# Mixer AB of a two-block network: order of the chunk-begin tables, engine of the chunk recurrence, place of the third responses

## The chip, the cores and the metric

One core of a Trainium2 chip runs the whole program. The metric is the time of one execution on the device in microseconds; the median of three runs of the kernel before is 2368.24 us.

## The reference, cut to what matters

Two blocks run one after the other on a sequence of 512 tokens with 1024 features. The first block has two layers; its layer 0 begins with the mixer below. The change touches only this mixer, and in it only the state-space part `s5_ssm` and the gates of the mLSTM part.

```python
def mixer_ab(x, ...):
    proj = x @ w_in                       # xm | zm | us, 512 columns each
    xc = silu(causal_dwconv(xm, conv_w, conv_b))
    q, k, v = block-diagonal products of xc, xc, xm
    gates = concatenate([q, k, v]) @ w_if + b_if
    h = mlstm_chunkwise(q, k, v, gates[:4], gates[4:])
    out_m = (layernorm(h) * mh_gain + skip * xc) * silu(zm)
    y = gelu(s5_ssm(us, ...))
    out_s = y * sigmoid(y @ w_glu + b_glu)
    return concatenate([out_m, out_s]) @ w_out

def s5_ssm(u, ...):                       # 32 groups of 64 complex states
    x[t] = ab * x[t-1] + bb @ u[t]        # ab, bb from a, dt, b
    y[t] = re(c @ x[t]) + d * u[t]
```

## The kernel before, in words

Every projection is made of three TensorE passes in a split format: a weight tile `raw` of 128x1024 is loaded by the SP queue (three buffers), ScalarE rounds it to `wh` (line 142), VectorE takes the rest `wl = raw - wh` (line 145), and lines 269 to 271 multiply. `fill(zm, n)` runs n steps of three such matmuls of the projection `zm`; the mixer puts them between its small products.

The state-space part cuts the 512 tokens into 64 chunks of 8. It needs two sets of tables, both products of powers of `ab` (`par`, `pai`) with `b` or `c`:

- `end_state_tables` (line 891) makes `zr`, `zi` on VectorE, four groups of four columns of groups. Per group, six instructions of 128x512: two products into a PSUM tile `aux`, two into `zr` and `zi`, and two sums. The powers lie in PSUM too (tile `chain`), so each instruction has at least one input in PSUM.
- `start_state_tables` (line 909) makes `cr`, `ci` on POOL in two halves. Per half, six instructions of 128x1152 with both inputs in SBUF (four products, two sums), and a negation on ScalarE. They read the reversed powers `pcr`, `pci`, which ScalarE copies out of `par`, `pai`.

Then `end_transpose` and `end_states` (lines 923 and 933) turn `zr`, `zi` on TensorE and give every chunk's end state `X`, in four groups; `conv` (line 987) makes one quarter of `xc` beside each: a ScalarE instruction, three VectorE instructions with both inputs in SBUF (`ta`), a ScalarE Silu. The work tiles `ta` have two buffers, shared by the turned tables and the convolution. `scan` (line 945) is the recurrence over the 64 chunks: on POOL, 28 instructions of 128x256 inside blocks of eight chunks, 28 of 128x32 across the blocks (`cy`), and then twelve VectorE and four POOL instructions that make the chunks' begin states `Xp`.

`responses` (line 995, four calls) multiplies `cr`, `ci` with `zr`, `zi` on TensorE (32 matmuls) and has ScalarE copy the result to `hs`, of which there is one buffer: `hs0` for calls 0 and 1, `hs1` for calls 2 and 3. `toeplitz` (line 1009, two calls) adds the skip weights on VectorE and spreads `hs` by 16 transfers on the SP queue into `Mt`. `block_diag` makes the block-diagonal weights `bd` with twelve VectorE instructions, in the buffer that `zr` had. The heads come behind: `head_decay` (decay weights `wt`), `values`, `queries_keys`, `head_scores`, `head_b`, `head_c`, and between them `ssm_out`, which reads `Mt`, `Xp`, `cr`, `ci`.

TensorE's order in the mixer is the order of the program, written out by hand (`manual_schedule`). On the other engines a planner orders the instructions: it walks a timeline of its own, and each engine takes the first in the program among those ready. `issue_after(ins)` makes the instructions traced under it stand behind `ins` on the engine of `ins`. The program's order around the change is: `xm` projection, end and start tables, chunk powers on POOL, first step of `zm`, the four groups with the convolution, `scan`, responses 0, gate matmuls (line 1201, which read all four quarters of `xc`), gate arithmetic, responses 1, `toeplitz(0)`, running sum and maximum of the gates (`fr`, `mr`, lines 1232 and 1234), gate transposes (lines 1241, 1242), responses 2 and 3, `toeplitz(1)`, `block_diag`, the last fills, heads.

Of the kernel before, what the change touches and what calls it, by code (L numbers as in the profile page):

```python
# [131 lines left out]
def tile_blocks(ctx: ExitStack, tc: tile.TileContext, A: dict, P: dict, off: dict, cst: bass.AP, out: bass.AP):  # L132
# [11 lines left out]
    def tt(out, a, b, op=ALU.mult, eng=None):  # L144
        return (eng or V).tensor_tensor(out=out, in0=a, in1=b, op=op)  # L145
# [24 lines left out]
    def chain_tile():  # L170
        return aux_p.tile([128, 512], F32, tag="chain", name="chain", bufs=1)
# [509 lines left out]
    def mixer_ab(scr_u):  # L681
        W = A["ab_w_in"][0]
        with tc.tile_pool(name="ab", bufs=1) as mp, tc.tile_pool(name="abt", bufs=2) as tp:
            def slot(i, shape, nm, dt=F32):
                return mp.tile(shape, dt, tag=f"s{i}", name=nm)
# [61 lines left out]
            def block_diag(out, nm):  # L747
                wr = vpart(nm).rearrange("p (m e) -> p m e", m=4)
                for m in range(4):
                    tt(out[:, m].rearrange("p (n e) -> p n e", e=4), blk4.rearrange("p (n e) -> p n e", e=4),  # L750
                       wr[:, m:m + 1, :].to_broadcast([128, 32, 4]))
# [17 lines left out]
            with tc.issue_after(last_split.ins):  # L769
# [51 lines left out]
                def powers(eng, pr, pi, order):  # L821

                    for t in (1, 2, 4):
                        cmul(eng, pr[:, :, order(t + 1, 2 * t + 1)], pi[:, :, order(t + 1, 2 * t + 1)],
                             pr[:, :, order(1, t + 1)], pi[:, :, order(1, t + 1)],
                             b_(pr[:, :, order(t, t + 1)], t), b_(pi[:, :, order(t, t + 1)], t), pt1[:, :, 0:t], pt2[:, :, 0:t])
# [63 lines left out]
            def end_state_tables():  # L890


                pw = chain_tile()[:, 0:288].rearrange("p (i j t) -> p i j t", i=2, j=16)
                act(pw[:, 0], par)
                act(pw[:, 1], pai)
                bbr, bbi, b1, b2 = (s5b[:, 1024 + i * 256:1280 + i * 256].rearrange("p (j q) -> p j q", q=16) for i in range(4))
                g16r, g16i = (b_(c.rearrange("p (j a) -> p j a", a=1), 16) for c in (gr, gi))
                cmul(V, bbr, bbi, bre, bim, g16r, g16i, b1, b2)
                for b4 in range(4):
                    js = slice(b4 * 4, b4 * 4 + 4)  # L900
                    pr, pi = pw[:, 0, js, 1:9], pw[:, 1, js, 1:9]
                    for z, p0, p1, op in ((zr, pr, pi, ALU.subtract), (zi, pi, pr, ALU.add)):
                        t = aux_tile().rearrange("p (j q s) -> p j q s", j=4, q=16)
                        outer(V, t, bbi[:, js], p1, 8, True)
                        outer(V, z[:, js], bbr[:, js], p0, 8, True)
                        tt(z[:, js], z[:, js], t, op)

            def start_state_tables():

                for hj in range(2):  # L910
                    eng = G
                    tc_ = slot(8 + hj, [128, 8, 9, 16], "tc")
                    js = slice(hj * 8, hj * 8 + 8)
                    outer(eng, cr[:, js], cre[:, js], pcr[:, js], 9, False)
                    outer(eng, tc_, cim[:, js], pci[:, js], 9, False)
                    tt(cr[:, js], cr[:, js], tc_, ALU.subtract, eng=eng)
                    outer(eng, ci[:, js], cre[:, js], pci[:, js], 9, False)
                    outer(eng, tc_, cim[:, js], pcr[:, js], 9, False)
                    tt(ci[:, js], ci[:, js], tc_, ALU.add, eng=eng)
                    act(ci[:, js], ci[:, js], scale=-1.0)  # L920
# [23 lines left out]
            def scan():  # L944

                Xv = X.rearrange("p i j (b r) -> p i j b r", r=8)
                a8s = mp.tile([128, 2, 16], F32, name="a8s")
                ts(a8s[:, 0], pwi[:, :, 1], -1.0, eng=G)
                G.tensor_copy(out=a8s[:, 1], in_=pwi[:, :, 1])
                sh = [128, 2, 16, 8]  # L950
                A8r = pwr[:, :, 1:2].rearrange("p (i j) b -> p i j b", i=1).to_broadcast(sh)
                A8i = a8s.rearrange("p i (j b) -> p i j b", b=1).to_broadcast(sh)
                sct = ev.tile([128, 512], F32, tag="sq", name="sct")
                t, u = (sct[:, i * 256:(i + 1) * 256].rearrange("p (i j b) -> p i j b", i=2, j=16) for i in range(2))
                for r in range(1, 8):
                    tt(t, Xv[:, :, :, :, r - 1], A8r, eng=G)
                    tt(u, Xv[:, ::-1, :, :, r - 1], A8i, eng=G)
                    tt(t, t, u, ALU.add, eng=G)
                    tt(Xv[:, :, :, :, r], Xv[:, :, :, :, r], t, ALU.add, eng=G)
                cy = ev.tile([128, 2, 16, 8], F32, tag="rbm", name="cy")  # L960
                G.memset(cy[:, :, :, 0], 0.0)
                w1, w2 = t[:, :, :, 0], u[:, :, :, 0]
                p8s = mp.tile([128, 2, 16], F32, name="p8s")
                ts(p8s[:, 0], pwi[:, :, 8], -1.0, eng=G)
                G.tensor_copy(out=p8s[:, 1], in_=pwi[:, :, 8])
                p8r = pwr[:, :, 8:9].rearrange("p j i -> p i j").to_broadcast([128, 2, 16])
                for b in range(1, 8):
                    tt(w1, cy[:, :, :, b - 1], p8r, eng=G)
                    tt(w2, cy[:, ::-1, :, b - 1], p8s, eng=G)
                    tt(w1, w1, w2, ALU.add, eng=G)  # L970
                    tt(cy[:, :, :, b], w1, Xv[:, :, :, b - 1, 7], ALU.add, eng=G)
                for hj in range(2):
                    js = slice(hj * 8, hj * 8 + 8)
                    for i in range(2):
                        Xp[i, hj] = resid.tile([128, 8, 64], F32, tag=f"xh{4 + i * 2 + hj}", name=f"Xp{i}{hj}")
                        o = Xp[i, hj].rearrange("p j (b r) -> p j b r", r=8)
                        t = sct.rearrange("p (j b r) -> p j b r", j=8, b=8)
                        cyr, cyi = (cy[:, c, js].rearrange("p j (b a) -> p j b a", a=1).to_broadcast([128, 8, 8, 8]) for c in range(2))
                        pr, pi = (w[:, js, 0:8].rearrange("p j (a r) -> p j a r", a=1).to_broadcast([128, 8, 8, 8])
                                  for w in ((pwr, pwi) if i == 0 else (pwi, pwr)))  # L980
                        tt(o, cyr, pr)
                        tt(t, cyi, pi, eng=G)
                        tt(o, o, t, ALU.subtract if i == 0 else ALU.add)
                        tt(o[:, :, :, 1:8], o[:, :, :, 1:8], Xv[:, i, js, :, 0:7], ALU.add)

            def conv(m):
                cw, cb = cols["ab_conv_w"], cols["ab_conv_b"]
# [161 lines left out]
            with tc.manual_schedule(engines={T.engine}):  # L1149
# [5 lines left out]
                ci = slot(5, [128, 16, 9, 16], "ci")  # L1155
                pc = ev.tile([128, 3, 16, 9], F32, tag="sq", name="pc")
                pcr, pci, pwr = (pc[:, i] for i in range(3))
                for t in range(9):
                    act(pcr[:, :, t], par[:, :, 8 - t])
                    act(pci[:, :, t], pai[:, :, 8 - t])  # L1160
                with tc.issue_after(last_split.ins):
                    end_state_tables()
                    start_state_tables()

                G.memset(pwr[:, :, 0], 1.0)
                G.memset(pwi[:, :, 0], 0.0)
                G.tensor_copy(out=pwr[:, :, 1], in_=par[:, :, 0])
                G.tensor_copy(out=pwi[:, :, 1], in_=pai[:, :, 0])
                powers(G, pwr, pwi, lambda lo, hi: slice(lo, hi))
                sz = slot(7, [128, 4, 512], "sz")  # L1170
                zm = proj_fine([(W, 512 + c * 128, ev_zm(c)) for c in (0, 2)], xh, xl, KD)

                def fill(gen, n):
                    for _ in range(n):
                        next(gen, None)
# [7 lines left out]
                for b4 in range(4):  # L1183
                    conv(b4)
                    end_states(b4)
                    if b4 < 3:
                        end_transpose(b4 + 1)
                        fill(zm, 2)
                scan()


                Mt = [slot(8 + i, [128, 16, 128], f"Mt{i}") for i in range(2)]
# [43 lines left out]
                tt(er, fr, mr, ALU.add)  # L1236
                ts(mr, mr, -1.0)
                fill(zm, 4)
                ps = chain_tile()
                for tb in range(NT):  # L1240
                    T.transpose(ps[:, tb * 4:tb * 4 + 4], cr4[:, tb * 128:(tb + 1) * 128], ident[0:4, 0:4])
# [2 lines left out]
                em = mp.tile([128, NT, 4], F32, name="em")  # L1244
                V.tensor_copy(out=cc.rearrange("p a b -> p (a b)"), in_=ps[:, 0:16])
                act(em.rearrange("p a b -> p (a b)"), ps[:, 16:32], AF.Exp, scale=-1.0)
                hsl[1] = mp.tile([128, 8, 8, 16], F32, tag="hs", name="hs1")
                responses(2)
                fill(zm, 2)
                responses(3)  # L1250
                toeplitz(1)
                bd = slot(0, [128, 3, 4, 128], "bd")
                for i, nm in enumerate(("ab_wv", "ab_wq", "ab_wk")):
                    block_diag(bd[:, (2, 0, 1)[i]], nm)
                q = [resid.tile([128, 512], F32, tag=f"xh{m}", name=f"q{m}") for m in range(4)]
                kk_ = [resid.tile([128, 512], F32, tag=f"xl{m}", name=f"k{m}") for m in range(4)]
                v = slot(1, [128, 2112], "v")[:, 0:NT * 516].rearrange("p (t m e) -> p t m e", t=NT, m=4)
# [620 lines left out]
```

## Time and profile before

| what | us |
|---|---|
| median of 3 runs (2367.17 to 2369.4) | 2368.24 |
| the profiled execution | 2366.72 |
| its span, first to last instruction | 2364.6 |
| TensorE busy in the span | 2309.1 (98%) |
| VectorE busy | 1363.6 (58%) |
| ScalarE busy | 1033.1 (44%) |
| POOL busy | 461.6 (20%) |

The profile is of one execution. PE is TensorE, DVE VectorE, ACT ScalarE, POOL GpSimd, SP the queue of loads. Times are counted from the first instruction. Busy shares are averages over the span; a stage is read from the stretch where it lies. The mean granted clock of TensorE is 0.994 of 2.4 GHz.

### The profile page before, as it was taken

How to read it: one execution, taken by the hardware profiler on the slowest of the kernel's cores; microseconds unless marked ns; L12 is line 12 of the kernel's file. 1: busy time of each engine (PE TensorE's matmuls, PEld its weight loads, DVE VectorE, ACT ScalarE, POOL GpSimd, SP SyncE). 2: the span in 40 equal slices, each digit the busy share in tenths (PEclk: the TensorE clock that was granted, in tenths of full speed). 3: DMA queues.
4: the chain of work that ended last, by engine and by line, in shares of the span. 5: the costliest groups of instructions: out<-in, count | busy, mean ns of one | idle time of the engine just before them, and what ended most of it. 6: DMA issues, size and time to landing. Idle time of an engine off the chain costs nothing.

```text
span 2364.6 us, 30936 instructions
## 1 busy us (share of the span) xinstructions
PE 2309.1 (98%) x12106; PEld 1929.7 (82%) x12106; DVE 1363.6 (58%) x2054; ACT 1033.1 (44%) x1583; POOL 461.6 (20%) x519
## 2 busy tenths in 40 slices
PE   9799999999999999999999999999999999999999
PEld 7558888888878888888888778888888878888888
DVE  8675744432657556444228675777533775777722
ACT  4545533222568554323235664444323573444411
POOL 5831400001401132000017562000002662000000
PEclk9899999999999999999999999999999999999999
DMA  6212333323332223333334103333234203333332
GB/s 189 62 22 71 99 98 99 98 90 112 107 89 72 72 90 99 97 94 95 98 98 132 57 28 98 101 96 98 94 98 120 82 2 98 98 98 98 94 116 94
DMA packets 204609, 216.04 MB, mean 91 GB/s; under 512 B 11888, under 2 KB 189936, under 8 KB 204464
## 3 DMA queue, kind: packets, MB, share of 16 engines
q1 hardware_dynamic: 204464, 214.08, 29.4%
q8 instruction: 95, 1.56, 0.3%
q14 instruction: 50, 0.41, 0.1%
HBM read 209.72 MB, written 3.15 MB: 90 GB/s over the span
## 4 chain that ended last, share of the span: by engine, by line
PE 83%; DVE 7%; POOL 4%; ACT 3%; issue 2%; DMA 0%; SPq 0%; DVEq 0%; ACTq 0%; POOLq 0%
PE mm L271 21%; PE mm L269 21%; PE mm L270 21%; PE mm L313 5%; PE mm L445 2%; PE mm L446 2%; PE mm L447 2%; DVE wl L145 1%; DVE xl L148 1%; PE aux L1662 1%; PE chain L1686 1%; POOL ra L145 1%; PE mm L1641 1%; ACT L142 1%; ACT wh L142 1%
## 5 line engine op out<-in xcount | busy, mean ns | idle before, releaser
L145 DVE TENSOR_TENSOR wl<-raw,wh 128x1024 fp32r<-128x1024 f32 (+1 forms) x396 | 492.0, 1243 | 615.8 <-ACT wh L142 614.8
L142 ACT ACTIVATE wh<-raw 128x1024 fp32r<-128x1024 f32 (+1 forms) x396 | 411.7, 1040 | 721.2 <-PE mm L270 525.4
L269 PE MATMUL mm<-xh,wh 128*128 128x512 f32 x1536 | 602.1, 392 | 0.5 <-ACT xh L142 0.5
L270 PE MATMUL mm<-xl,wh 128*128 128x512 f32 x1536 | 599.2, 390 | 2.4 <-DVE xl L148 2.4
L271 PE MATMUL mm<-xh,wl 128*128 128x512 f32 x1536 | 598.7, 390 | 2.1 <-DVE wl L145 2.0
L270 PEld LDWEIGHTS mm<-xl,wh 128*128 128x128 f32 x1536 | 289.1, 188 | 63.4 <-DVE xl L148 4.2
L271 PEld LDWEIGHTS mm<-xh,wl 128*128 128x128 f32 x1536 | 288.9, 188 | 63.0 <-DVE wl L145 3.0
L269 PEld LDWEIGHTS mm<-xh,wh 128*128 128x128 f32 x1536 | 289.1, 188 | 62.0 <-issue 1.7
L145 POOL TENSOR_TENSOR acc<-acc,sq 128x256 f32<-128x256 f32 (+1 forms) x77 | 86.6, 1124 | 418.9 <-issue 263.7
L145 POOL TENSOR_TENSOR accm<-accm,sq 128x512 f32<-128x512 f32 (+1 forms) x24 | 32.1, 1338 | 677.3 <-ACT sq L142 677.0
L148 DVE SCALAR_TENSOR_TENSOR y<-cbuf,vec,y 128x512 f32<-128x512 f32 x176 | 131.1, 748 | 38.0 <-ACT y L142 35.9
L445 PE MATMUL mm<-wh,xh 128*128 128x512 f32 (+1 forms) x384 | 147.7, 385 | 0.1
L446 PE MATMUL mm<-wh,xl 128*128 128x512 f32 (+1 forms) x384 | 143.9, 375 | 0.0
L447 PE MATMUL mm<-wl,xh 128*128 128x512 f32 (+1 forms) x384 | 143.8, 375 | 0.0
L270 PE MATMUL mm<-bl,wh 128*128 128x512 f32 x308 | 119.8, 389 | 0.0
L269 PE MATMUL mm<-bh,wh 128*128 128x512 f32 x308 | 119.8, 389 | 0.0
L271 PE MATMUL mm<-bh,wl 128*128 128x512 f32 x308 | 119.8, 389 | 0.0
L142 ACT ACTIVATE y<-cbuf,vec 128x512 f32<-128x512 f32 x88 | 71.4, 813 | 98.5 <-DVE cbuf L145 96.5
L269 PE MATMUL mm<-gh,wh 128*128 128x512 f32 x264 | 102.7, 389 | 0.0
L271 PE MATMUL mm<-gh,wl 128*128 128x512 f32 x264 | 102.7, 389 | 0.0
L270 PE MATMUL mm<-gl,wh 128*128 128x512 f32 x264 | 102.7, 389 | 0.0
L145 DVE TENSOR_TENSOR t<-mm,rb 128x512 f32<-128x512 f32 (+1 forms) x92 | 58.4, 642 | 58.7 <-PE mm L271 58.4
(465 smaller groups left out, 3847.1 us busy)
## 6 DMA issues: line engine op xcount, KB each, us to landing
raw<-in_ffn_w SPq DMA_DIRECT2D x136, 512.0 KB, 3.6
raw<-in_w_up SPq DMA_DIRECT2D x88, 512.0 KB, 3.5
raw<-in_w_down SPq DMA_DIRECT2D x43, 512.0 KB, 3.5
raw<-in_c_w_in SPq DMA_DIRECT2D x33, 512.0 KB, 3.8
raw<-in_w_in SPq DMA_DIRECT2D x31, 512.0 KB, 3.7
raw<-in_w_o SPq DMA_DIRECT2D x16, 512.0 KB, 3.6
raw<-in_ab_w_in SPq DMA_DIRECT2D x11, 512.0 KB, 5.0
raw<-in_ab_w_out SPq DMA_DIRECT2D x9, 512.0 KB, 3.6
```

Of the source, the lines that this page charges most:

```text
L142: S.activation(out=out, in_=in_, func=func, scale=scale, **kw)
L145: return (eng or V).tensor_tensor(out=out, in0=a, in1=b, op=op)
L148: return V.scalar_tensor_tensor(out=out, in0=a, scalar=s, in1=b, op0=op0, op1=op1)
L269: T.matmul(ps, h, xh, start=first, stop=False)
L270: T.matmul(ps, h, xl, start=False, stop=False)
L271: T.matmul(ps, l, xh, start=False, stop=last)
L313: T.matmul(o, w[:, k, m * 128:(m + 1) * 128], x, start=k0 == mine[0] and k == 0 and p == 0, stop=k0 == mine[-1] and k == nk - 1 and p == 2)
L445: T.matmul(o, xh[:, sl], wh[:, k, :], start=first, stop=False)
L446: T.matmul(o, xl[:, sl], wh[:, k, :], start=False, stop=False)
L447: T.matmul(o, xh[:, sl], wl[:, k, :], start=False, stop=last)
L1641: T.matmul(sc, qT[:, h, sl], kT[c][:, h // 4, :], start=c == 0, stop=c == 1)
L1662: T.transpose(pt[:, kb * 128:(kb + 1) * 128], p[:, kb * 128:(kb + 1) * 128], ident)
```

## The change

Four edits, all in the mixer. The chunk powers on POOL stand ahead of the start tables in the program, and the end tables are traced first; the last of the nine columns of `pcr` and `pci` is no longer copied by ScalarE but by two VectorE copies that stand behind the last end-table instruction, so that POOL's first table product, which reads all nine, waits for them. The 56 instructions of the recurrence run on VectorE in place of POOL. The third responses (call 2) and their buffer come ahead of the gate transposes on TensorE. The second Toeplitz and the block diagonals stand behind the last instruction of the recurrence on VectorE.

```diff
@@ end_state_tables
-                        tt(z[:, js], z[:, js], t, op)
+                        last = tt(z[:, js], z[:, js], t, op)
+                return last
@@ scan
                 for r in range(1, 8):
-                    tt(t, Xv[:, :, :, :, r - 1], A8r, eng=G)
-                    tt(u, Xv[:, ::-1, :, :, r - 1], A8i, eng=G)
-                    tt(t, t, u, ALU.add, eng=G)
-                    tt(Xv[:, :, :, :, r], Xv[:, :, :, :, r], t, ALU.add, eng=G)
+                    tt(t, Xv[:, :, :, :, r - 1], A8r)
+                    tt(u, Xv[:, ::-1, :, :, r - 1], A8i)
+                    tt(t, t, u, ALU.add)
+                    tt(Xv[:, :, :, :, r], Xv[:, :, :, :, r], t, ALU.add)
...
                 for b in range(1, 8):
-                    tt(w1, cy[:, :, :, b - 1], p8r, eng=G)
-                    tt(w2, cy[:, ::-1, :, b - 1], p8s, eng=G)
-                    tt(w1, w1, w2, ALU.add, eng=G)
-                    tt(cy[:, :, :, b], w1, Xv[:, :, :, b - 1, 7], ALU.add, eng=G)
+                    tt(w1, cy[:, :, :, b - 1], p8r)
+                    tt(w2, cy[:, ::-1, :, b - 1], p8s)
+                    tt(w1, w1, w2, ALU.add)
+                    carried = tt(cy[:, :, :, b], w1, Xv[:, :, :, b - 1, 7], ALU.add)
...
+                return carried
@@ mixer_ab
-                for t in range(9):
+                for t in range(8):
                     act(pcr[:, :, t], par[:, :, 8 - t])
                     act(pci[:, :, t], pai[:, :, 8 - t])
-                with tc.issue_after(last_split.ins):
-                    end_state_tables()
-                    start_state_tables()
 
                 G.memset(pwr[:, :, 0], 1.0)
                 G.memset(pwi[:, :, 0], 0.0)
                 G.tensor_copy(out=pwr[:, :, 1], in_=par[:, :, 0])
                 G.tensor_copy(out=pwi[:, :, 1], in_=pai[:, :, 0])
+                with tc.issue_after(last_split.ins):
+                    last_end = end_state_tables()
                 powers(G, pwr, pwi, lambda lo, hi: slice(lo, hi))
+
+                with tc.issue_after(last_end.ins):
+                    V.tensor_copy(out=pcr[:, :, 8], in_=par[:, :, 0])
+                    V.tensor_copy(out=pci[:, :, 8], in_=pai[:, :, 0])
+                start_state_tables()
...
-                scan()
+                carried = scan()
...
                 fill(zm, 4)
+                hsl[1] = mp.tile([128, 8, 8, 16], F32, tag="hs", name="hs1")
+                responses(2)
                 ps = chain_tile()
...
                 act(em.rearrange("p a b -> p (a b)"), ps[:, 16:32], AF.Exp, scale=-1.0)
-                hsl[1] = mp.tile([128, 8, 8, 16], F32, tag="hs", name="hs1")
-                responses(2)
                 fill(zm, 2)
                 responses(3)
-                toeplitz(1)
                 bd = slot(0, [128, 3, 4, 128], "bd")
-                for i, nm in enumerate(("ab_wv", "ab_wq", "ab_wk")):
-                    block_diag(bd[:, (2, 0, 1)[i]], nm)
+                with tc.issue_after(carried.ins):
+                    toeplitz(1)
+                    for i, nm in enumerate(("ab_wv", "ab_wq", "ab_wk")):
+                        block_diag(bd[:, (2, 0, 1)[i]], nm)
```

## Rows read from the trace of the kernel before

**Rows 1.** Stretches: length, each engine's busy time (instructions), granted clock, DMA share, GB/s
```profile
58.00:72.00 14.00, 5.84 (x26) 3.87 (x26) 14.00 (x13) 2.85 (x4) 14.00 (x9) 0.63 0.23 76
...
68.30:71.50 3.20, 3.18 (x10) 2.57 (x10) 3.20 (x3) 0.60 (x1) 3.20 (x3) 0.51 0.11 38
...
136.30:139.80 3.50, 3.50 (x5) 1.51 (x6) 3.03 (x7) 1.21 (x4) 1.55 (x3) 0.52 0.00 0
```
**Rows 2.** TensorE's waits between 36 and 150 us: total, times, longest
```profile
PE aux L927 <- DVE zr L145: 5.5, 1, 5.5
PE chain L1242 <- DVE fr L145: 4.1, 1, 4.1
PE aux L1025 <- DVE wt L145: 2.4, 2, 1.3
PE mm L271 <- DVE wl L145: 2.0, 1, 2.0
PE chain L1201 <- ACT xc L142: 0.9, 1, 0.9
...
PE aux L927 <- DVE zi L145: 0.7, 1, 0.7
```
**Rows 3.** Timeline of VectorE, 35 to 70 us: start, length
```profile
35.75 0.22 DVE L145 TENSOR_TENSOR pt<-par 128x64 f32<-128x64 f32 x1
...
36.02 0.42 DVE L145 TENSOR_TENSOR s5b<-s5b 128x256 f32<-128x256 f32 x1
...
38.38 2.29 DVE L145 TENSOR_TENSOR s5b<-s5b 128x256 f32<-128x256 f32 x1
40.59 2.17 DVE L145 TENSOR_TENSOR pai<-pt,pt 128x64 f32<-128x64 f32 x1
42.68 1.21 DVE L145 TENSOR_TENSOR wl<-raw,wh 128x1024 fp32r<-128x1024 f32 x1
...
48.60 2.95 DVE L145 TENSOR_TENSOR wl<-raw,wh 128x1024 fp32r<-128x1024 f32 x1
...
57.45 3.03 DVE L145 TENSOR_TENSOR wl<-raw,wh 128x1024 fp32r<-128x1024 f32 x1
...
62.80 3.08 DVE L145 TENSOR_TENSOR wl<-raw,wh 128x1024 fp32r<-128x1024 f32 x1
...
68.79 0.67 DVE L145 TENSOR_TENSOR zi<-zi,aux 128x512 f32<-128x512 f32 x1
```
**Rows 4.** Groups of POOL by form, 36 to 145 us: count, busy, mean ns
```profile
L145 POOL TENSOR_TENSOR tc<-s5b,pc 128x1152 f32<-128x1152 f32 x4 | 8.5, 2140 | 0.0
...
L145 POOL TENSOR_TENSOR ci<-ci,tc 128x1152 f32<-128x1152 f32 x2 | 5.2, 2631 | 0.0
```
**Rows 5.** Groups of VectorE by form, 36 to 145 us
```profile
L145 DVE TENSOR_TENSOR aux<-s5b,chain 128x512 f32<-128x512 f32 x8 | 5.5, 681 | 0.0
...
L145 DVE TENSOR_TENSOR lg<-lg,le 128x16 f32<-128x16 f32 x1 | 0.7, 712 | 0.0
```
**Rows 6.** Timeline of VectorE, 72 to 130 us
```profile
72.37 0.74 DVE L148 SCALAR_TENSOR_TENSOR ta<-xm,vec,ta 128x512 f32<-128x512 f32 x1
...
85.73 3.21 DVE L148 SCALAR_TENSOR_TENSOR ta<-xm,vec,ta 128x512 f32<-128x512 f32 x3
...
115.97 3.87 DVE L145 TENSOR_TENSOR bd<-blk,vec 128x128 f32<-128x128 f32 x12 [0.28 <-PE aux L1003]
...
129.48 0.75 DVE L145 TENSOR_TENSOR Xp<-cy,pc 128x512 f32<-128x512 f32 x1 [1.16 <-POOL cy L145]
```
**Rows 7.** Timeline of POOL: the recurrence's second and last instruction
```profile
87.18 1.21 POOL L145 TENSOR_TENSOR sct<-X,a8s 128x256 f32<-128x256 f32 x1
...
129.14 0.30 POOL L145 TENSOR_TENSOR cy<-sct,X 128x32 f32<-128x32 f32 x1
```
**Rows 8.** Timeline of ScalarE: the last quarter of xc
```profile
88.97 0.63 ACT L142 ACTIVATE xc<-ta 128x512 f32<-128x512 f32 x1 [1.14 <-DVE ta L148]
```
**Rows 9.** The chain that ended last: the third responses
```profile
109.32 3.36 PE aux L1003 x32
```

## The prediction

> **What bounds the kernel now.** TensorE is busy for 98% of the span (the table above), so time can be won only where it waits or runs at its lower clock, and the change touches the stretch from 36 to 148 us alone. I read that stretch in four views. The stretches with their granted clock come first [rows 1]: between 58 and 72 us TensorE has 5.8 us of work in 14.0. TensorE's waits say who ended them [rows 2]: the first hole is a wait for the weight split `wl` (2.0) and for VectorE's chunk-end tables `zr` (5.5, and 0.7 more for `zi`); the second is the gate's running sums (`fr`, 4.1). Two smaller ones are the causal convolution's last `xc` (0.9) and, among the heads, the decay weights `wt` (2.4 in two waits, the longer 1.3). After two of these the granted clock is 0.51 and 0.52, which is 1.2 GHz, for 3.2 and 3.5 us [rows 1].
>
> VectorE's timeline says why the tables are late [rows 3]. The split of 128x1024 takes 1.21 us, but three of them in the tables' stretch take 2.95 to 3.08, one 128x256 product 2.29 instead of 0.42, one 128x64 sum 2.17 instead of about 0.22. Each has both inputs in SBUF and meets one of POOL's 128x1152 instructions (2.14 to 2.63 us, twelve of them in the chunk-begin tables) [rows 4]. The chunk-end tables' own instructions take an input from PSUM; their eight `aux` products take 0.68 us in the mean, with POOL busy beside them [rows 5]. So today POOL's tables lie beside VectorE work that mostly does not feel them.
>
> **The change, part by part**
>
> *POOL waits for VectorE.* Five stretched instructions lose their wait: 1.9 + 1.9 + (2.95 + 3.03 + 3.08 - 3 x 1.21 = 5.4) = 9.2 us. The last table instruction then starts at 59.6 instead of 68.79 [rows 3] and ends at 60.2. TensorE is through its xm products at 58 in either kernel, where the hole begins, so it would lose 8.2 us of waits (2.0 + 5.5 + 0.7) and 1.6 us of slow clock (half of 3.2 [rows 1]): 9.8 us on offer. POOL's 18 small power instructions run earlier beside PSUM-fed work, and two of 18 ScalarE copies become two VectorE copies of 16 columns: nothing, at most 0.4 us.
>
> *What is late next.* POOL's twelve table instructions start at about 60.4: 8 x 2.14 + 4 x 2.63 = 27.7 us if alone. Beside them VectorE now has the convolution: twelve 128x512 `ta` instructions and a split `wl`, all with two SBUF inputs. Alone a `ta` takes 0.74 us; three beside POOL's short 128x256 instructions took 3.21, and one of POOL's between them 1.21: they take turns [rows 6, 7]. Against 128x1152 instructions each `ta` waits 2.14 to 2.63 first. In turns: the split to 61.5, POOL's 27.7, eleven instructions of 0.65 between them (7.2), the last `ta` 0.74 and ScalarE's 0.63 for `xc`: the last `xc` at 97.8 instead of 89.6 [rows 8]. Fewer turns give 96.5, another split in the row 99.5. All gate matmuls stand behind that `xc` on TensorE, whose order is fixed; so the 9.8 us on offer are not kept, and the gate comes **8.2 us later** (6.9 to 9.9). The first responses wait for POOL's first six table instructions and ScalarE's negation, at 60.4 + 1.1 + 13.9 + 5 x 0.65 = 79 at the earliest; that lies under the longer wait.
>
> The Trainium skill, SBUF — State Buffer, section "Who interferes with whom", says the shared pair goes to whichever instruction starts first and "Issue order, not op shape, decides who blocks". Read so that VectorE's queued instructions keep the pair, the convolution would run at 0.74 us each and the sum would be that of the first rival; the rows of turn-taking above speak against that reading.
>
> *Clock.* TensorE now waits 0.9 us before the gate [rows 2]; it would come there up to 9.8 earlier and leave 8.2 later, so it idles some 10 us. The nearest rows cost 1.6 and 1.7 us of half rate after a hole [rows 1]; ends 0 and 1.7. **+1.6**.
>
> *Recurrence on VectorE.* POOL loses 56 instructions, spread from before 87.2 to 129.4 [rows 7]. No row shows them on VectorE. The near rows are the 128x256 product (0.42) and a 128x64 one (0.22) [rows 3]; most need the one before, so no overlap: 28 x 0.42 + 28 x 0.22 = 18 us, between 12 (all at 0.22) and 24 (all at 0.42). They follow the convolution, from 97 to about 122 with other work between, so they share VectorE with the gate's ten small instructions. Each of these may stand behind one recurrence instruction, up to 0.4 each (+4), and no longer meets POOL's 128x256 ones (a sum of 16 columns, `lg`, took 0.71 [rows 5], 0.5 more than the 0.22 of 64 columns; for six such, -3). **+1** (-3 to +4).
>
> *Third responses in the gate gap.* 32 matmuls, two ScalarE copies, no DMA. They take 3.36 us at half clock behind the gap [rows 9], so 1.7 in it at full clock, under the 4.1 us wait. What is left of the gap, some 3 us, is still more than the 1.3 us after which the clock fell among the heads [rows 1, 2], so I let the slow stretch move to what follows. **-1.7** (0 if the gap has closed; -3.4 if the clock stays up). The two copies must wait until the first Toeplitz transfers have read the one `hs` buffer; they hold one `aux` bank meanwhile, and nobody needs the result before the second Toeplitz.
>
> *Second Toeplitz and block diagonals behind the recurrence.* The block diagonals already wait for the fourth responses (they start at 115.97, 3.87 us for twelve) [rows 6] and would start at about 122 to 124 in either case; the cover is the last fill of TensorE, about 5 us; without it up to 4 us. The 16 Toeplitz transfers stay in front of the output-weight loads on SP, as now, and these are needed only after the heads. **0** (to +4).
>
> *Heads.* The chunk states' twelve `Xp` instructions leave the stretch from 129.48 on [rows 6], where they stand between the decay weights: waits of 2.4 and half clock for 3.5 us (1.7) [rows 1, 2]. They now run at some 122 to 131, before the first `wt` product. **-3.5** of 4.1 (0 to -4.1).
>
> *Sum*: 8.2 + 1.6 + 1 - 1.7 - 3.5 = **+5.6 us**. Made against the profiled execution: 2366.7 + 5.6 = 2372.3; the median of the runs (2368.24) stands 1.5 above that execution, so **2373.8** for a median. Work behind the heads is bound by TensorE and moves with it. The bounds together give -4 (6.9 + 0 - 3 - 3.4 - 4.1) to +20 (9.9 + 1.7 + 4 + 0 + 4 + 0), neither end likely whole; the likeliest case by itself is 2367 to 2380. What a measurement of this kernel can tell from no change is about 0.2%, or 4.7 us.
>
> **The rivals**
>
> *VectorE keeps the port (faster).* If its back-to-back instructions go first and POOL only fits in between, the convolution is hidden as now, the first responses come at 76 and the gate at about 80. Then -9.6 + 1 - 1.7 - 3.5 = -13.8: 2354. The Trainium skill's sentence on issue order, named above, is what would allow it. For it: nothing in the rows is an exact pair of a 128x512 `ta` and a 128x1152 table instruction. Against it: the turns in [rows 6, 7] and the one whole wait of each split [rows 3]. It decides at the mean time of a `ta`: (97.8 - 0.6 - 61.5) / 12 = 2.97 us in my sum, break-even 5.6 us earlier, at 2.5, and faster beyond the limit of measurement under 2.1. Chance 0.18, halves of it included.
>
> *The gate queues behind the whole recurrence (slower still).* The planner orders VectorE by program order among what it takes to be ready, and the recurrence stands ahead of the gate. The gate's first VectorE instruction, `ga`, would be asked for at about 104 (some 6 us of matmuls behind `xc` at 97.8); behind all 56 it runs at 97 + 18 = 115. About +10 more: 2384. For it: the program order. Against it: in the profile VectorE's order mixes chains, since a dependent instruction leaves room for another. Chance 0.15.
>
> *The waits do nothing.* The wait on the recurrence may be idle, as the block diagonals wait anyway. The wait of POOL can't be: the two copies feed POOL's first product. So the whole edit is not without effect, but its parts can cancel (gate +6.9, clock +1.6, heads -4.1, gap -3.4): +1, about 2369. That is the forecast's lower part and gets no chance of its own.
>
> **How the numbers follow.** Forecast 0.67, of which 0.37 lies more than 4.7 us above, 0.28 within, 0.02 below. The first rival gives 0.18 faster; the second 0.13 slower and 0.02 within. Faster 0.20, same 0.30, slower 0.50. The range leaves out a tenth at each end: the lower part of the first rival, and the end of the second: 2360 to 2381.
>
> **What would show it.** Right: the three splits at 1.2 us and the last `zi` at 60; TensorE's 5.5 us wait for `zr` gone; twelve `ta` of 2.5 to 3.3 us between POOL's table instructions; the largest wait of the stretch now at the gate matmuls, for `xc`, 8 to 14 us, ending at 96 to 100; the wait for `fr` shorter by 1.7; no `Xp` between the `wt`. Wrong: `ta` near 0.8 beside POOL's tables, or the gate matmuls before 90 us; or a recurrence that holds `ga` for 10 us.

## The result, and the profile after

The changed kernel takes 2388.08 us (median of four runs, 2387.18 to 2389.64) where the one before takes 2367.99 beside it: ratio 1.0087, 95% interval 1.0075 to 1.0100. That is **20.1 us slower**, where 5.6 were forecast. The profiled execution's span is 2386.4 us, 21.8 above that of before.

TensorE's timeline locates the loss. Before (the last gate matmuls, the transposes of `lf`, `head_decay(0)`, `ssm_out(0)`):

```profile
90.12 1.44 PE L1201 MATMUL chain<-xm,wg 128*32 128x512 f32 x5
...
99.96 0.60 PE L1229 MATMUL aux<-ident,lf 128*4 128x128 f32 x4
...
121.06 1.12 PE L1040 MATMUL chain<-mr,ident 4*128 4x512 f32 x2
...
148.38 0.44 PE L1117 MATMUL aux<-Mt,U 128*64 128x128 f32 x4
```

And after (first, the responses between which it stops):

```profile
79.84 0.41 PE L1005 MATMUL aux<-cr,zr 64*16 64x128 f32 x4
98.30 0.61 PE L1005 MATMUL aux<-ci,zi 64*16 64x128 f32 x4 [18.05 <-ACT ci L142]
...
105.14 1.04 PE L1207 MATMUL chain<-xm,wg 128*32 128x512 f32 x8
...
123.52 1.01 PE L1235 MATMUL aux<-ident,lf 128*4 128x128 f32 x4 [8.78 <-DVE lf L145]
...
140.34 1.12 PE L1042 MATMUL chain<-mr,ident 4*128 4x512 f32 x2
...
170.07 0.44 PE L1119 MATMUL aux<-Mt,U 128*64 128x128 f32 x4
```

The gate matmuls end 14.6 us later (106.18 against 91.56), `lf` is turned 23.6 later, the heads begin 19.3 later, `ssm_out(0)` 21.7 later; from there to the end the distance hardly moves. So there are two losses (14.6 at the responses, 8.9 at `lf`), one gain of 4.3 between `lf` and the heads, and a last loss of 2.4 in the heads. TensorE's waits between 36 and 190 us name the first two, where before it waited for `zr` and `fr` [rows 2]:

```profile
PE aux L1005 <- ACT ci L142: 18.1, 1, 18.1
PE aux L1235 <- DVE lf L145: 8.8, 1, 8.8
PE aux L940 <- ACT ta L142: 5.0, 2, 3.6
```

The stretches that answer to [rows 1] show the clock: the hole at 58 to 72 is filled, and the new one has 5.7 us of work in 14 at half clock.

```profile
58.00:72.00 14.00, 10.37 (x122) 8.37 (x122) 12.35 (x11) 8.12 (x13) 12.06 (x5) 0.93 0.19 59
72.00:90.00 18.00, 6.92 (x74) 5.61 (x70) 16.49 (x7) 6.17 (x10) 18.00 (x7) 0.69 0.04 11
90.00:104.00 14.00, 5.70 (x34) 3.75 (x34) 13.59 (x20) 4.63 (x6) 7.01 (x4) 0.50 0.08 26
104.00:120.00 16.00, 10.75 (x81) 7.47 (x80) 14.07 (x45) 1.74 (x4) 1.10 (x1) 0.93 0.00 0
```

Why `ci` is late: POOL's timeline, then ScalarE's.

```profile
59.94 5.65 POOL L145 TENSOR_TENSOR cr<-s5b,pc 128x1152 f32<-128x1152 f32 x2 [13.07 <-ACT ta L142]
65.55 2.60 POOL L145 TENSOR_TENSOR tc<-s5b,pc 128x1152 f32<-128x1152 f32 x1
...
75.76 6.11 POOL L145 TENSOR_TENSOR cr<-cr,tc 128x1152 f32<-128x1152 f32 x2
81.83 5.13 POOL L145 TENSOR_TENSOR tc<-s5b,pc 128x1152 f32<-128x1152 f32 x2
86.92 6.60 POOL L145 TENSOR_TENSOR ci<-ci,tc 128x1152 f32<-128x1152 f32 x2
...
95.81 0.63 ACT L142 ACTIVATE xc<-ta 128x512 f32<-128x512 f32 x1 [8.39 <-DVE ta L148]
96.47 0.72 ACT L142 ACTIVATE ta<-xc,vec 128x512 f32<-128x512 f32 x1
97.10 2.20 ACT L142 ACTIVATE ci<-ci 128x1152 f32<-128x1152 f32 x2
```

POOL doesn't finish one half and then the other: the planner runs each kind of instruction for both halves, so the first half's sum `ci` is the eleventh of twelve, done at about 90.5. Its negation then stands on ScalarE behind the last quarter's Silu (95.81), and the first responses get it at 98.3. Why `lf` is late, on VectorE:

```profile
59.04 0.67 DVE L145 TENSOR_TENSOR zi<-zi,aux 128x512 f32<-128x512 f32 x1
...
59.80 1.21 DVE L145 TENSOR_TENSOR wl<-raw,wh 128x1024 fp32r<-128x1024 f32 x1
60.94 7.75 DVE L148 SCALAR_TENSOR_TENSOR ta<-xm,vec,ta 128x512 f32<-128x512 f32 x3
70.23 6.11 DVE L148 SCALAR_TENSOR_TENSOR ta<-xm,vec,ta 128x512 f32<-128x512 f32 x3 [1.54 <-ACT ta L142]
...
84.88 3.16 DVE L145 TENSOR_TENSOR wl<-raw,wh 128x1024 fp32r<-128x1024 f32 x1
87.97 6.10 DVE L148 SCALAR_TENSOR_TENSOR ta<-xm,vec,ta 128x512 f32<-128x512 f32 x2
93.99 0.60 DVE L145 TENSOR_TENSOR sct<-X,pc 128x256 f32<-128x256 f32 x1
...
116.54 0.22 DVE L145 TENSOR_TENSOR cy<-sct,X 128x32 f32<-128x32 f32 x1
...
118.72 0.18 DVE L145 TENSOR_TENSOR ga<-chain,vec 128x32 f32<-128x32 f32 x1
...
140.04 1.28 DVE L145 TENSOR_TENSOR Xp<-cy,pc 128x512 f32<-128x512 f32 x2
```

The tables end where forecast (`zi` starts at 59.04; [rows 3] had 68.79), the convolution's twelve `ta` take 2.5 us each in the median (a row gives the time of all its instructions together; the first of the row at 70.23 met only the end of a POOL instruction and took 1.00, the one alone behind POOL's tables 0.73), and the whole recurrence, 93.99 to 116.76, stands ahead of `ga`, whose matmuls ended near 108.6.

### The profile page after: what moved, and what is told of

Same layout as the page of the kernel before. It is cut to its first block, busy times and chain, and to the rows that moved or that the text cites. A ratio compares the mean times of both kernels' runs of the same rounds, so it can differ in the third digit from the quotient of the medians.

```text
span 2386.4 us, 30941 instructions
## 1 busy us (share of the span) xinstructions
PE 2315.9 (97%) x12106; PEld 1934.7 (81%) x12106; DVE 1387.9 (58%) x2112; ACT 1034.2 (43%) x1581; POOL 429.6 (18%) x463
## 4 chain that ended last, share of the span: by engine, by line
PE 83%; DVE 7%; POOL 4%; ACT 3%; issue 2%; SPq 1%; DMA 0%; ACTq 0%; POOLq 0%; DVEq 0%
PE mm L271 21%; PE mm L269 21%; PE mm L270 21%; PE mm L313 5%; PE mm L445 2%; PE mm L446 2%; PE mm L447 2%; DVE wl L145 1%; DVE ta L148 1%; PE aux L1669 1%; PE chain L1693 1%; POOL ra L145 1%; PE mm L1648 1%; ACT L142 1%; ACT wh L142 1%
## 5 line engine op out<-in xcount | busy, mean ns | idle before, releaser
L145 POOL TENSOR_TENSOR acc<-acc,sq 128x256 f32<-128x256 f32 (+1 forms) x77 | 87.3, 1134 | 418.4 <-issue 263.7
```

## The experiments

Starts on TensorE in us, and the wait for `ci` at the first responses:

| kernel | wait `ci` | `lf` turned | head_decay(0) | ssm_out(0) | time |
|---|---|---|---|---|---|
| before | 0 | 99.96 | 121.06 | 148.38 | 2367.99 |
| changed | 18.1 | 123.52 | 140.34 | 170.07 | 2388.08 |
| tables_only | 16.5 | 112.81 | 134.57 | 161.26 | 2379.41 |
| recurrence_only | 0 | 102.41 | 125.49 | 156.03 | 2372.94 |
| responses_only | 0 | 100.17 | 119.38 | 144.75 | 2363.20 |
| conv_in_psum | 10.8 | 117.63 | 134.19 | 164.13 | 2382.26 |
| first_half_first | 6.6 | 116.09 | 133.23 | 160.58 | 2378.81 |
| gate_ahead | 17.1 | 112.57 | 133.60 | 173.73 | 2391.24 |
| gate_ahead_bd | 17.1 | 112.97 | 134.48 | 162.49 | 2382.71 |
| recurrence_pool | 15.8 | 112.20 | 132.99 | 160.91 | 2381.50 |
| combo_v | 12.2 | 89.97 | 120.77 | 154.01 | 2373.29 |
| combo_g | 6.6 | 92.02 | 119.26 | 150.41 | 2369.08 |
| gate_early | 0 | 97.91 | 114.61 | 142.59 | 2363.44 |
| fill_early | 0 | 98.82 | 115.95 | 149.81 | 2370.52 |

Ratios with intervals stand below for the five that were timed nine or ten times; the others are single runs. The kernel before, beside each group of four kernels, had medians of 2367.72, 2367.12 and 2367.39 us; in the second group its 18 times lay between 2365.85 and 2370.52, so a difference of 2 or 3 us between single runs says little.

### The parts alone

**tables_only**: the kernel before with the waits of POOL's tables and nothing else of the change.

```diff
+                with tc.issue_after(last_split.ins):
+                    last_end = end_state_tables()
...
+                with tc.issue_after(last_end.ins):
+                    V.tensor_copy(out=pcr[:, :, 8], in_=par[:, :, 0])
+                    V.tensor_copy(out=pci[:, :, 8], in_=pai[:, :, 0])
+                start_state_tables()
```

> Only POOL's wait for VectorE's tables; recurrence on POOL and third responses where they were. Theory (the convolution and POOL's late tables take turns at the port, and the gate stands behind both): the same turns of some 2.5 us per convolution instruction, the first responses wait for ScalarE's ci until about 98, the gate comes 14 to 15 us later than before, and the whole is 13 to 18 us slower. Rival (the recurrence on VectorE is what costs): within 3 us of before.

11.7 us slower, 1.3 under the bottom of the forecast. TensorE waits 16.5 us for `ci`, and with the recurrence on POOL it doesn't wait for `lf`. This part loses the most.

**recurrence_only**: the kernel before with the 56 recurrence instructions on VectorE.

```diff
-                    tt(t, Xv[:, :, :, :, r - 1], A8r, eng=G)
+                    tt(t, Xv[:, :, :, :, r - 1], A8r)
```

> Only the 56 recurrence instructions on VectorE; POOL's tables early as before. Theory: the gate is then in time to be interleaved with the recurrence, so the running sum is later by at most 3 us; the wait for lf stays under 3 us; total -2 to +4 us. Rival (the recurrence costs its 18 us wherever it runs ahead of the gate): about +9 us, with the wait for lf of some 9 us as in the changed kernel.

Ratio 1.0021 (1.0012 to 1.0031), 5.2 us slower, just over the forecast's upper end. Here the gate's few instructions stand between the recurrence's (`ga` at 95.61, `lf` at 102.18), since the gate is ready early. Of the 7.7 us by which `ssm_out(0)` is late, 2.5 are there at `lf`; the rest comes behind.

**responses_only**: the kernel before with the third responses ahead of the gate transposes.

```diff
                 fill(zm, 4)
+                hsl[1] = mp.tile([128, 8, 8, 16], F32, tag="hs", name="hs1")
+                responses(2)
                 ps = chain_tile()
```

> Only the third responses ahead of the gate transposes. Theory: they fill 1.7 us of the 4.1 us wait and run at full clock, 2 to 4.5 us faster. Rival (their copies to the one hs buffer wait for the first Toeplitz transfers and hold ScalarE's queue up): within 1.5 us of before, with a wait of ScalarE for Mt<-hs of about 3 us.

Ratio 0.9980 (0.9971 to 0.9989), **4.5 us faster**. TensorE's wait for `fr` falls from 4.1 to 2.9 us, and the granted clock between 120 and 148 is 1.00, where it was 0.94.

### The first loss: the turns and the order on POOL

**conv_in_psum**: the changed kernel, with the convolution's work tile in PSUM, so that its VectorE instructions have one input in SBUF.

```diff
-                t = tmp()
+                t = mm_tile()
                 act(t, xm[:, m, 3:515], AF.Identity, ...)
```

> The changed kernel with the convolution's work tile in PSUM, so its VectorE instructions have one input in SBUF. Theory: they take 0.75 us each beside POOL's tables, POOL's twelve instructions end at about 88 instead of 93.5, the first responses stop waiting at about 90 instead of 98, the recurrence's first instructions now meet the tables in their place, and the total is about +8 to +13 us over before instead of +20. Rival (the port is not the cause, only the order of the queues): the convolution still takes 2 us or more each and the total stays within 3 us of the changed kernel.

5.8 us faster than the changed kernel, still 14.5 above before: 1.5 over the theory's range, and not the rival. VectorE's timeline:

```profile
64.24 7.66 DVE L148 SCALAR_TENSOR_TENSOR mm<-xm,vec,mm 128x512 f32<-128x512 f32 x10
...
75.80 2.92 DVE L145 TENSOR_TENSOR sct<-X,pc 128x256 f32<-128x256 f32 x1
78.65 2.89 DVE L145 TENSOR_TENSOR sct<-X,a8s 128x256 f32<-128x256 f32 x1
```

Ten convolution instructions in a row take 0.77 each beside POOL's tables, so the turns are shown. The recurrence then comes early and takes the turns instead: 2.9 us for what took 0.60 in the changed kernel. POOL's tables end at 91.4, where the theory had 88, and `ga` still stands behind all 56 (wait for `lf` 12.0 us, although the gate matmuls end at 97.1). Beside the wait for `ci` the first responses wait 4.0 us for `cr`. The edit does a second thing: the convolution no longer shares the two `ta` buffers with the turned tables. How the 5.8 us divide between the two was not tried.

**first_half_first**: the changed kernel, with POOL's second half held behind the first half's last sum.

```diff
+                done0 = None
                 for hj in range(2):
+                  with tc.issue_after(done0.ins) if hj else nullcontext():
...
-                    tt(ci[:, js], ci[:, js], tc_, ALU.add, eng=eng)
+                    done0 = tt(ci[:, js], ci[:, js], tc_, ALU.add, eng=eng)
```

> The changed kernel, with POOL's six table instructions of the second half held until the first half's last sum (ci) is issued; nothing else is touched. Theory (the first responses waited for a sum that stood eleventh of twelve on POOL, and for its negation queued on ScalarE behind the last Silu): the first half is done after six instructions in turns with conv, near 78 us, its negation goes ahead of the last Silu, and TensorE's wait at the first responses falls from 18.1 us to under 3; the gate's matmuls then wait for conv's last channel (96 us) instead, and end near 99; with the recurrence still mostly ahead of ga, lf's transposes start at 113 to 118 us and the time is 2378 to 2383. Rival (the port alone sets it: conv is as late as the tables, so the wait only changes its name): the gate's matmuls end at 104 or later and the time is 2385 to 2389.

9.3 us faster than the changed kernel, inside the theory's range, though the wait for `ci` was forecast at under 3 us. The first half's sum ends at 77.15, but the negation comes later, on ScalarE:

```profile
85.38 0.63 ACT L142 ACTIVATE xc<-ta 128x512 f32<-128x512 f32 x1 [3.91 <-DVE ta L148]
86.62 0.71 ACT L142 ACTIVATE ta<-xc,vec 128x512 f32<-128x512 f32 x1
87.71 1.15 ACT L142 ACTIVATE ci<-ci 128x1152 f32<-128x1152 f32 x1
```

It is queued behind the third quarter's Silu, so 6.6 us of the wait are left. With it gone from the front, the gate matmuls wait 1.4 us for `xc`, whose Silu starts at 96.36, and end at 98.95: the wait that I had forecast as the longest is there, and lay hidden under the responses'. This run shows the order of the tables as a cause; conv_in_psum shows the turns. It also bears on the second loss. The gate is early here, and yet `ga` stands behind 24 recurrence instructions, 8.2 us after its matmuls, and TensorE waits about as long for `lf` as in the changed kernel (timelines of TensorE and VectorE, then TensorE's wait):

```profile
100.37 0.95 PE L1215 MATMUL chain<-sel,tb 128*128 128x8 f32 x8
...
109.00 0.62 DVE L145 TENSOR_TENSOR X<-X,sct 128x256 f32<-128x256 f32 x1
109.53 0.18 DVE L145 TENSOR_TENSOR ga<-chain,vec 128x32 f32<-128x32 f32 x1
...
PE aux L1237 <- DVE lf L145: 8.6, 1, 8.6
```

### The second loss: the recurrence ahead of the gate

**gate_ahead**: the changed kernel, with the recurrence held behind `lf`.

```diff
+                lf_done = tt(lf, lf, lg, ALU.subtract)
+                with tc.issue_after(lf_done.ins):
+                    carried = scan()
```

> The changed kernel, with the 56 recurrence instructions on VectorE held until the gate's last VectorE instruction (lf) is issued; the tables, the third responses and everything else stay. Theory (the gate's arithmetic waited behind the whole recurrence): TensorE's wait of 8.8 us for lf goes to under 1 us; the gate's matmuls still end at about 106 us, because the first responses still wait some 18 us for POOL's ci; lf's transposes start at about 114 to 116 us instead of 123.5, and the time is 2379 to 2382 us, 6 to 9 below the changed kernel. Rival (the recurrence, now 20 us later, is itself needed soon): its 23 us end near 138 us, the carried state and the heads' tables on VectorE queue behind it, and 3 us or less of the 8.8 are left at the first ssm_out: 2385 to 2388.

`lf` is turned 11 us earlier with no wait, and yet the time is 3 us longer: outside both forecasts. TensorE's waits hold a new row:

```profile
PE aux L1036 <- DVE bd L145: 12.1, 2, 11.3
```

The change holds `bd` behind the recurrence's last instruction, which now ends at 144.3; `bd` starts at 145.66 instead of 135.24, and the values wait for it.

**gate_ahead_bd**: the same without that rule for `toeplitz(1)` and `bd`.

```diff
-                with tc.issue_after(carried.ins):
-                    toeplitz(1)
+                toeplitz(1)
```

> The run with the gate ahead of the recurrence, without the rule that holds the second Toeplitz matrix and the 12 instructions of the head matrices bd behind the recurrence. Theory (that run lost its gain of 11 us at lf because bd, behind the recurrence, kept TensorE waiting for 12.1 us at the values): the wait for bd is under 2 us, head_decay(0) stays near 133.6 us, ssm_out(0) comes at 161 to 165 instead of 173.7, and the time is 2378 to 2383 us. Rival (the 23 us of the recurrence still hold Xp, which no order on VectorE avoids): the wait moves to ssm_out(0), 168 or later, and the time is 2385 to 2390.

The wait for `bd` is gone, `ssm_out(0)` comes 11.2 us earlier than in gate_ahead, and the time is 5.4 below the changed kernel, at the theory's upper end. So the rule, at which I had put nothing, costs nothing only as long as the recurrence is early.

**recurrence_pool**: the changed kernel with the recurrence back on POOL and nothing held behind it.

```diff
-                    tt(t, Xv[:, :, :, :, r - 1], A8r)
+                    tt(t, Xv[:, :, :, :, r - 1], A8r, eng=G)
...
-                with tc.issue_after(carried.ins):
-                    toeplitz(1)
+                toeplitz(1)
```

> The changed kernel with the recurrence put back on POOL, and so nothing for the second Toeplitz matrix and the head matrices to be held behind; the waits of POOL's tables and the third responses stay. Theory (the parts don't add: alone the tables cost 11.7 us, the recurrence 5.2 and the third responses -4.5, together 12.4, while the change costs 20 to 21; the rest is the recurrence standing ahead of a gate that the tables have made late): the wait of 8.8 us for lf is gone, and the time is what tables and responses give alone, 2373 to 2377 us, so that the recurrence costs 11 to 15 us in the changed kernel where it cost 5 in the one before. Rival (the rest is in the tables and the heads, not in the recurrence): 2380 to 2384.

14.1 us above the kernel before, 6.0 less than the change: the rival's forecast. By the times the recurrence with its rule costs 6.0 here and 5.2 alone; by the starts of `ssm_out(0)` it is 9.2 here and 7.7 alone. So it is the smaller share of what the parts cost more together. The larger is the third responses' missing gain: from tables_only this kernel differs in effect by them alone, and its `ssm_out(0)` is only 0.35 us earlier, where the same move alone made it 3.6 earlier. The granted clock between 120 and 148 is 0.82 (0.87 in tables_only). The 2.4 us by which this run is the longer lie behind the mixer: at about 276 us, in the next projection, it is still the earlier (12.5 behind before, tables_only 13.5). Both are single executions.

### Towards a better kernel

**combo_v**: the changed kernel with four edits: convolution in PSUM, POOL's first half first, gate matmuls ahead of the first responses, recurrence behind `lf`. New beside the diffs above:

```diff
-                responses(0)
-                fill(zm, 2)
                 ps = chain_tile()
...
+                responses(0)
+                fill(zm, 2)
                 responses(1)
```

> The changed kernel with four edits: conv's work tile in PSUM, POOL's second half of the tables behind the first, the gate's matmuls ahead of the first responses in TensorE's order, and the recurrence on VectorE behind lf. Theory (the change's own early splits and early end-state tables are worth some 9 us, and were lost to the turns on the port, to the order of POOL's tables and to the recurrence ahead of the gate): conv ends near 76 us, the gate's matmuls run at 77 to 84, lf's transposes start at 91 to 97 us (99.96 before), the third responses give their 4 us, and the time is 2352 to 2362 us, below the kernel before. Rival (the recurrence, later still in the queue, holds the carried state and the heads, or POOL's second half at 91 us holds the third responses): head_decay(0) is earlier but ssm_out(0) is not, and the time is 2364 to 2372.

Ratio 1.0026 (1.0016 to 1.0036): what the rival describes, 1.3 us over its range. `lf` is turned at 89.97, ten us before the kernel before, but the next wait takes its place: with the gate out of the way TensorE waits 12.2 us for `ci`, and `bd` stands behind the recurrence on VectorE (`cy` ends at 121.2, `bd` starts at 122.58; 114.32 in responses_only).

**combo_g**: the same with the recurrence on POOL and nothing held behind it.

```diff
+                    tt(t, Xv[:, :, :, :, r - 1], A8r, eng=G)
...
+                toeplitz(1)
```

> The changed kernel with conv's work tile in PSUM, POOL's second half behind the first, the gate's matmuls ahead of the first responses, and the recurrence back on POOL with nothing held behind it. Theory (what the run of the four edits lost between head_decay(0) at 120.8 us and ssm_out(0) at 154.0, 33 us instead of the 27 of before, is the recurrence on VectorE): the recurrence on POOL begins at 91 us and its carried state ends at 125 to 135; bd is ready by 115, ssm_out(0) comes at 145 to 150, and the time is 2364 to 2370 us: no better than the kernel before, because POOL's tables now end 20 us later than before. Rival (with everything else early, POOL hidden behind the heads): 2356 to 2363.

As in the theory, 1.7 us above the kernel before, and some 4 below combo_v. POOL's carried state ends at 138.9, where it ended at 129.4 [rows 7]: the tables start some 22 us later than before, and the recurrence's instructions, though the first starts at 83.23, stand on POOL among those of the tables' second half, which ends at 95.4.

**gate_early**: the kernel before with the third responses moved, the convolution in PSUM, and the gate matmuls ahead of the first responses.

```diff
-                t = tmp()
+                t = mm_tile()
...
-                responses(0)
-                fill(zm, 2)
                 ps = chain_tile()
```

> The kernel before with three edits: the third responses in the gate gap (alone worth 4.5 us), conv's work tile in PSUM, and the gate's matmuls ahead of the first responses in TensorE's order; POOL's tables stay beside VectorE's, the recurrence stays on POOL. Theory (before, conv's last channel at 89 us is late only because conv is queued on VectorE behind tables that end at 72 us): the gate's matmuls end 1 to 3 us earlier and the time is 2360 to 2363, hardly below the third responses alone. Rival (conv out of the shared interface frees more, since its last channel stood beside POOL's recurrence): 2354 to 2359.

Ratio 0.9982 (0.9973 to 0.9992), 3.7 us faster, 0.4 over the theory's range. `ssm_out(0)` is 2.2 us ahead of responses_only; in the medians no difference is left.

**fill_early**: the same with six fill steps moved from ahead of the `lf` transposes to ahead of the first end-state transposes.

```diff
-                fill(zm, 1)
+                fill(zm, 7)
                 end_transpose(0)
...
                 toeplitz(0)
-                fill(zm, 6)
```

> The kernel before with the third responses in the gate gap, conv's work tile in PSUM, the gate's matmuls ahead of the first responses, and six of zm's fill steps moved from ahead of lf's transposes to ahead of the first end-state transposes. Theory (TensorE's idle time and low clock at 60 to 72 us, while it waits for zr, can take the six steps, and the gate, whose lf is ready some 4 us before its transposes, comes forward by what they took): lf's transposes start near 94 us instead of 97.9, and the time is 2357 to 2361. Rival (zm's second weights aren't split yet, or the heads are bound by POOL's carried state at 124 us): the wait changes its name, 2362 to 2365.

Ratio 1.0014 (1.0004 to 1.0024): slower, outside both forecasts. `lf` is turned no earlier, since the last gate matmuls ended 3.6 us later than in gate_early. `head_decay(0)` is 1.3 later, `ssm_out(0)` 7.2; the carried state on POOL ends 7.9 later, and the granted clock between 120 and 148 is 0.77 instead of 1.00. Which of the two holds the heads was not taken apart.

The best is the third responses alone, or gate_early, which equals it within its interval: both beat both kernels.

## Why the prediction was wrong

The sign was right, the size was not: 20.1 us against 5.6, past the range's end of 2381.

*Right.* The splits take 1.21 us, the 5.5 us wait for `zr` is gone, the tables end 9.7 us earlier, and the convolution takes turns with POOL's tables: the last `xc` ends at 96.4 (97.8 forecast). The first rival is out: VectorE did not keep the port. Its sign was badly chosen, though: the mean of the twelve `ta` is 2.3 us, under the 2.5 named as break-even, and the last `xc` is late all the same, because the split at 84.88 takes a turn too (3.16) and VectorE waits twice for ScalarE (1.5 and 1.4). The prediction read the Trainium skill's page SBUF — State Buffer, section "Who interferes with whom", as a possible case for VectorE keeping the shared pair. The traces show turns instead: with both queues full, VectorE and POOL alternate one for one, as the `ta` above against POOL's instructions of 2.6 us show. The rule of the same section of the Trainium skill, that an instruction of VectorE with at most one SBUF input, outside the 2-port perf modes, doesn't contend with POOL, agrees with conv_in_psum (0.77).

*The step that failed first*: "The first responses wait for POOL's first six table instructions and ScalarE's negation, at 60.4 + 1.1 + 13.9 + 5 x 0.65 = 79 at the earliest; that lies under the longer wait." The sum that they wait for is the eleventh instruction on POOL, not the sixth, and the negation stands behind the last Silu on ScalarE. I took the program's order of the halves for POOL's order. So the wait falls not at the gate but one response, one fill and 6 us of half-clock work ahead of it: +14.6 at the gate matmuls instead of +9.8 (8.2 and 1.6). That is 4.8 us past the forecast. first_half_first puts the gate back to 98.95, 7.4 later than before.

*The second*: recurrence, +1 forecast. The rival "the gate queues behind the whole recurrence" (+10 more, chance 0.15) came: 8.9 us at `lf`, 7.9 past the forecast and on TensorE's timeline the largest error. Its mechanism is the one written there, and the sign named for it, a recurrence that holds `ga` for 10 us, is in the trace (108.6 to 118.72). It doesn't need the first loss: in first_half_first the gate matmuls end at 98.95, earlier than the 101.4 that my sum gives, and the wait for `lf` is still 8.6. Where the recurrence starts at 87.3 and the gate matmuls end at 92.8 (recurrence_only) the two mix; where it is held behind `lf` (gate_ahead) the wait is gone. The 56 instructions take 23 us, near the upper bound of 24: 0.60 to 0.65 for three in four of those of 128x256, which no row showed, and 0.42 for the fourth.

*Third responses*: from the `lf` transposes to `head_decay(0)` the changed kernel takes 16.8 us instead of 21.1, a gain of 4.3 where 1.7 was taken, and the wait for `fr` is gone. The third responses alone don't give that: the same stretch takes 19.2 in responses_only and 20.8 in recurrence_pool. It is 16.6 to 17.1 in the changed kernel, conv_in_psum and first_half_first, where most or all of the recurrence on VectorE lies ahead of `lf`, and 21.0 where it lies behind (gate_ahead). So most of this gain goes with the early recurrence, which costs the 8.9 us.

*Heads*: -3.5 forecast, +2.4 came. `Xp` didn't go ahead to 122 to 131: the first of them starts at 140.04. They stand on VectorE behind `bd` and the second `hs` sums, and use the buffers of the inputs (`xh`) that `zm`'s last fills read until 140.4. In conv_in_psum, first_half_first and recurrence_only too the first `Xp` starts within 0.5 us of `head_decay(0)`, which follows the last fill; the term did not reckon with those buffers. Which of the two held them was not tried, so the cause stays open. ScalarE's writes of `hs` waited for the first Toeplitz transfers (3.0 us), which came late with `lf`. The clock is 0.85 between 120 and 180, where it was 0.97.

The account, one part on top of the other: by times, tables 11.7, third responses 2.4, recurrence with its rule 6.0, together 20.1; by the starts of `ssm_out(0)`, 12.9, -0.4 and 9.2, together 21.7. The two differ behind the mixer, in single runs, so the second is the better measure of the parts.

## What to carry to other kernels

An order that is written as a loop is not the order of an engine whose instructions a planner places: before costing "the first half", read in the planned or traced order where its last instruction stands, and which queue the instruction behind it sits in. A move that shortens one wait by ordering POOL's work behind VectorE's delays everything that POOL does later; here the tables started 22 us later to save 10. Where an engine takes over a long chain of work, see which short chain on it another engine waits for: with the recurrence held behind `lf` TensorE's wait of 8.8 us was gone, and with `bd` no longer held behind the recurrence the time was 5.4 us shorter. Take the parts of a change apart even when the sum is bad: the small one, third responses into an idle gap, is worth 4.5 us by itself.

## What the runs showed that I had not expected

- A VectorE instruction whose second input lies in PSUM isn't stretched by POOL (0.77 us against 2.5 in the median for the same step of the convolution), but the turns don't vanish: the next instruction in the queue with both inputs in SBUF takes them (2.9 us for 128x256, 0.60 alone).
- POOL pays too: its 128x1152 products take 2.14 us beside PSUM-fed work and 2.6 in turns with the convolution.
- The same 32 matmuls moved by one place gave more than the wait that they filled: 4.5 us from a wait that shrank by 1.2. Of the 3.6 us by which `ssm_out(0)` comes earlier, 1.7 are there at `head_decay(0)`. The rest lies in the heads, where in the one profiled execution of each kernel the granted clock between 120 and 148 is 1.00 (responses_only) instead of 0.94: the slow stretch at 136.3 of [rows 1] is missing. What keeps the clock up there was not tried.
